# Moving the SBUF tiles that TensorE reads onto multiples of 512 bytes, with the low halves of the weight splits 32 bytes off

## The chip, the cores and the metric

One core of one Trainium2 chip. The metric is the device time of one execution in microseconds; the kernel before takes 1749.63 us, the median of three runs (1748.19 to 1751.73).

## The reference, cut to what matters

Two layers of a hybrid transformer over 256 latent and 256 context tokens, model width 1024. Each layer is half-step SwiGLU, attention in three groups of heads, half-step SwiGLU, each behind a modulated RMS norm. Nearly all of the arithmetic is fp32 matrix products:

```python
def _swiglu(u, w_gate, w_up, w_down):
    return (jax.nn.silu(u @ w_gate) * (u @ w_up)) @ w_down
...
h = h + 0.5 * g1 * _swiglu(_modulate(_rms_norm(h, norm_ffn1[l]), sh1, sc1),
                           w_ffn1_gate[l], w_ffn1_up[l], w_ffn1_down[l])
...
p = u @ w_in[l]
...
h = h + gm * (jnp.concatenate([y_w, y_g, y_n], axis=-1) @ w_out[l])
```

with w_gate and w_up of 1024 x 2816 and w_down of 2816 x 1024, for both token sets (the last layer drops the context after its keys and values).

## The kernel before, in words

Everything stands transposed: features on the 128 partitions, tokens along them. To keep fp32 accuracy with fp32r products, each operand is split in a high and a low part and three products are accumulated, high x high, high x low, low x high (`mm3`, L129 to L132). One product is one weight load (128 x 128) and one matmul over 256 or 512 tokens, so TensorE works through a list of pairs "load, matmul" in program order; the load of the next pair runs beside the matmul of this one.

- **Weights.** `wload` (L122 to L127) brings 512 KB from HBM on SP's queue into a `raw` tile (3 buffers), ScalarE copies it, rounded, into the high half of a `split` tile (4 buffers), VectorE writes the difference into the low half. `w` in `first_tiles` does the same for the first six tiles of the first layer, four of them in `split` buffers and the last two (`split0`) in buffers of the G tag.
- **Moving operands.** The normalised activations are `Uh` and `Ul` (high and low, pool acts). A feed-forward stage makes `pg` and `pu` from them (gate and up), then the hidden tiles `G` (high and low side by side), from which `pd` (down) is made and added to `H`. The names `pq`, `pk`, `pv`, `S` and `po` are the products of the mixer (queries, keys, values, scores, outputs); its output product is again called `pd`, from `Uh` and `Ul`.
- **Order.** The steps of the first tiles and of the mixers stand in lists written out by hand (`START`, `MIX`); the feed-forward stages run in loops: chunk by chunk gate and up, after each part the down products of the part before. VectorE takes the modulation jobs (`ascr`, L147) between its other work.
- **Where tiles lie.** A pool's tiles stand one behind the other, and a pool opened later begins where the last one ended, so an address follows from the sizes and the order in which the pools are opened. Counted in bytes from the start of a partition, the kernel before has:

```
consts   16512 .. 25280    ident at 16512
weights  25280 .. 70336    raw 3 x 4096, then split 4 x 8192 from 37568 (low half at +4096)
acts     70336 .. 119488   H 70336, Uh 86720, Ul 103104
norm    119488 .. 125920   acc, ms, rs, sq, t, hms, hrs
stage   125920 ..          one pool per stage: ffn1_0, mix_0, ffn2_0, ffn1_1, mix_1, ffn2_1
```

25280, 37568, 86720 and 103104 are all 192 past a multiple of 512 and so on a multiple of 64. In the first stage a `csel` tile (4096) and a `c2` tile (64) stand ahead of G, which begins at 130080, 32 past a multiple of 512; in the other feed-forward stages G begins at 125920, 480 past one. Both are 32 past a multiple of 64. The tiles of the mixers' pool that TensorE reads are 480 past a multiple of 512 ahead of the `sm` tiles (3 x 64 bytes) and 160 past one behind them, again 32 past one of 64. Steps inside a tile are multiples of 512 bytes throughout.

Of the kernel before, what the change touches and what calls it, by code (L numbers as in the profile page):

```python
# [10 lines left out]
F32 = mybir.dt.float32  # L11
F32R = mybir.dt.float32r
# [7 lines left out]
KT = D // 128  # L20
# [2 lines left out]
A_H, B_H, C_H = 6, 4, 6  # L23
ABUFS = 8
DV = 6
BANKS = {"mm": 3, "s": 2, "t": 2, "o": 1}
PIECES = 4
NT0 = 6
# [31 lines left out]
def hybrid_backbone(ctx: ExitStack, tc: tile.TileContext, I, out):  # L60
    nc = tc.nc
    ep = ctx.enter_context
    cp = ep(tc.tile_pool(name="consts", bufs=1))
    wp = ep(tc.tile_pool(name="weights", bufs=4))
    up = ep(tc.tile_pool(name="acts", bufs=1))
    npl = ep(tc.tile_pool(name="norm", bufs=2))
    psum = ep(tc.tile_pool(name="psum", bufs=1, space=bass.MemoryType.PSUM))

    def bank(tag, name):
        return psum.tile([128, 512], F32, tag=tag, name=name, bufs=BANKS[tag])  # L70

# [49 lines left out]

    def wload(src, n=1024):  # L122
        raw = raw_load(src, n)
        sp = wp.tile([128, 2, 1024], F32R, tag="split", name="split", bufs=4)
        act(sp[:, 0, :n], raw[:, :n], AF.Copy)  # L125
        tt(sp[:, 1, :n], raw[:, :n], sp[:, 0, :n].bitcast(F32), ALU.subtract)  # L126
        return sp  # L127
# [129 lines left out]
    def first_tiles(pool, csel, U, src):  # L257

        pss, sps, rb, ada_ps, ada_pt, rstd, tmp = [], [], [], {}, {}, {}, {}

        def r(h):
            if not rb:
                rb.append(bank("o", "rb"))
            rstd[h] = norm_rstd_stages(h, rb[0], 256 * h, "mm")
            next(rstd[h])

        def s(h):
            next(rstd[h], None)  # L270

        def a(p, i):

            if i == 0:
                ada_ps[p] = bank("mm", "adaps")
            c, b = divmod(i, 2)
            raw = pool.tile([128, 4, 256], F32, tag="araw", name="araw", bufs=ABUFS)
            nc.sync.dma_start(raw, I["w_ada0"][:, p, c, b])
            for j in range(4):
                mm(ada_ps[p][32 * j:32 * j + 32, :256], csel[:, 2 * j + b, c, :], raw[:, j, :], start=(i == 0),  # L280
                   stop=(i == 3))

        def b(p):
            sb = pool.tile([128, 256], F32, tag="adasb", name="adasb", bufs=1)
            act(sb, ada_ps[p][:, :256], AF.Copy)
            pt = ada_pt[p] = bank("mm", "adapt")
            for i in range(2):
                nc.tensor.transpose(pt[:, i * 128:(i + 1) * 128], sb[:, i * 128:(i + 1) * 128], ident)

        def c(p):  # L290
            v = ada_pt[p][:, :256].rearrange("p (b j r) -> p b r j", b=2, j=4)
            for i in range(2):
                f = i * KT + 2 * p
                nc.vector.tensor_reduce(ada[0][:, f:f + 2, :], v[:, :, 2 * i:2 * i + 2, :], axis=AX.X, op=ALU.add)
            for m in ("sh1", "sc1"):
                ada_fin(0, m, 2, slice(2 * p, 2 * p + 2))

        def w(i):
            raw = raw_load(src(i), 1024)
            if i < 4:  # L300
                t = wp.tile([128, 2, 1024], F32R, tag="split", name="split", bufs=4)
                parts = [(t, 0, 1024)]
            else:
                parts = [(pool.tile([128, 2, 512], F32R, tag="G", name="split0", bufs=10), o, 512) for o in (0, 512)]
            for t, o, n in parts:
                act(t[:, 0, :], raw[:, o:o + n], AF.Copy)
            sps.append((raw, parts))

        def x(i):
            raw, parts = sps[i]  # L310
            for t, o, n in parts:
                tt(t[:, 1, :], raw[:, o:o + n], t[:, 0, :].bitcast(F32), ALU.subtract)
            pss.append(bank(("s", "t", "s", "t", "mm", "mm")[i], "pf"))

        def u(f):
            shv = mod(0, "sh1")
            t2 = pool.tile([128, 2, TOK], F32R, tag="G", name="t0", bufs=10)[:, 0, :].bitcast(F32)
            for h in range(2):
                cols = (LAT, CT)[h]
                t = tmp[f, h] = t2[:, cols]  # L320
                stt(t, H[:, f, cols], amod[0][:, 0, f, h:h + 1], rb[0][:, 256 * h:256 * h + 256], op0=ALU.mult,
                    op1=ALU.mult)
                marks["act"] = ins_of(act(U[0][:, f, cols], t, AF.Identity, bias=shv[:, f, h:h + 1]))

        def v(f):
            shv = mod(0, "sh1")
            for h in range(2):
                cols = (LAT, CT)[h]
                stt(U[1][:, f, cols], tmp.pop((f, h)), shv[:, f, h:h + 1], U[0][:, f, cols].bitcast(F32),
                    op0=ALU.add, op1=ALU.subtract)  # L330

        def m(i, f):
            t, o, _ = sps[i][1][f // 4 if i >= 4 else 0]
            wh, wl = (t[:, e, f * 128 - o:f * 128 - o + 128] for e in range(2))
            mm(pss[i], wh, U[0][:, f, :], start=(f == 0), stop=False)
            mm(pss[i], wl, U[0][:, f, :], start=False, stop=False)
            mm(pss[i], wh, U[1][:, f, :], start=False, stop=(f == KT - 1))

        steps = dict(r=r, s=s, a=a, b=b, c=c, w=w, x=x, u=u, v=v, m=m)
        with tc.manual_schedule():  # L340
            for o in START.split():
                steps[o[0]](*map(int, o[1:]))
        return pss
# [105 lines left out]
    def mixer(l, pool, U):  # L449
# [158 lines left out]

        def scores(g):
            kd_, h, kd, (q, rs), e, v, vh = head_info(g)  # L610
            sm = pool.tile([128, 4, 4], F32, tag="sm", name="sm", bufs=3)
            nm, sums, es, rr = (sm[:, i, :] for i in range(4))
            P = []
            st[g] = P
# [201 lines left out]
    for l in range(DEPTH):  # L816
        last = l == DEPTH - 1
        with tc.tile_pool(name=f"ffn1_{l}", bufs=1) as pool:
            start = None
            if l == 0:  # L820
                csel = pool.tile([128, KT, 4, 32], F32, name="csel")
                nc.gpsimd.memset(csel, 0.0)
                c2 = pool.tile([128, KT, 2], F32, name="c2")
                nc.sync.dma_start(c2, I["ccol"])
                for h in range(2):
                    for i in range(2):
                        w = slice(4 * i, 4 * i + 4)
                        nc.sync.dma_start(H[:, w, (LAT, CT)[h]], I["xT"][:, w, (LAT, CT)[h]])
                for i in range(4):
                    act(csel[:, :, i, 2 * i:2 * i + 2], c2, AF.Silu)  # L830
                for h in range(2):
                    for d in range(KT):
                        norm_sq(h, d, nc.vector, pool)
                U = new_u()

                def start(chunk):
                    return first_tiles(pool, csel, U, chunk)
            if l == 0:
                jobs = [late_consts] + ada_jobs(0, ("g1", "shm", "scm", "gm", "sh2", "sc2"), pool)
            else:  # L840
                jobs = ada_jobs(1, ("shm", "scm"), pool) + ada_jobs(1, ("gm", "sh2", "sc2", "g2"), pool, 1)
            Um = []
            ffn(l, 1, (0, 1), pool, U, jobs, next_u(l, 1, Um), start)
            U = Um
        halves = (0,) if last else (0, 1)
        with tc.tile_pool(name=f"mix_{l}", bufs=1) as pool:
            Y, qcols = mixer(l, pool, U)
            Um = []
            out_proj(l, halves, Y, qcols, next_u(l, 2, Um))
            U = Um  # L850
        with tc.tile_pool(name=f"ffn2_{l}", bufs=1) as pool:
            if not last:
                jobs = ada_jobs(0, ("g2",), pool) + ada_jobs(1, ("sh1", "sc1", "g1"), pool)
            else:
                jobs = []
            Um = []

            def final(h):
                rb = norm_rstd(0)
                for i in range(4):  # L860
                    t = pool.tile([128, 2, 256], F32, tag="fin", name="fin", bufs=4)
                    for d in range(2):
                        stt(t[:, d, :], H[:, 2 * i + d, LAT], gains[:, 6, 2 * i + d:2 * i + d + 1], rb,
                            op0=ALU.mult, op1=ALU.mult)
                    (nc.sync, nc.scalar)[i % 2].dma_start(out[:, 2 * i:2 * i + 2, :], t)
                return []

            ffn(l, 2, halves, pool, U, jobs, final if last else next_u(1, 0, Um))
            U = Um
# [75 lines left out]
```

## Time and profile before

| | |
|---|---|
| median of 3 runs | 1749.63 us |
| the profiled execution's own time | 1749.41 us |
| span of its trace | 1747.2 us |
| TensorE (matmuls) busy | 1707.2 us, 98% |
| VectorE busy | 1180.4 us, 68% |
| ScalarE busy | 718.0 us, 41% |
| mean granted TensorE clock | 0.994 of full speed |

A matmul's record runs from its start to its modelled end, and the next one starts long before that end. So busy time says only that TensorE is never empty; how fast it works is read from the distance between the starts of neighbouring matmuls, in the timeline.

### The profile page before, as it was taken

The page shows a single profiled execution, that of the slowest core. Times are in us where ns is not written, and L with a number is a line of the kernel's source. Part 1 is how long each engine was busy: PE and PEld are TensorE (multiplying, and loading weights), DVE is VectorE, ACT ScalarE, POOL GpSimd, SP SyncE. Part 2 cuts the span into 40 slices and gives each one's busy share as a digit, 9 for nine tenths or more (in the row PEclk, how much of TensorE's full clock was granted, in tenths as well). Part 3 has the DMA queues.
Part 4 walks back from the last instruction along what each step waited for, and adds up shares of the span by engine and source line. Part 5 has one row for each costly group of instructions (what it writes and reads, how often), then busy time and mean ns, then how long its engine had stood idle before and what let it go on. Part 6 is the DMA issues. An engine that isn't in the chain of part 4 may idle for free.

```text
span 1747.2 us, 24756 instructions
## 1 busy us (share of the span) xinstructions
PE 1707.2 (98%) x9572; PEld 1473.6 (84%) x9572; DVE 1180.4 (68%) x2031; ACT 718.0 (41%) x1206; POOL 167.3 (10%) x251
## 2 busy tenths in 40 slices
PE   7999999999999999999999999999999999989997
PEld 4888888889888898888888988888888888889997
DVE  5899963447888869983334599944333797965555
ACT  4322222235888643222222442222222477754443
POOL 0311100002101031100000121200000210210000
PEclk9999999999999999999999999999999999999999
DMA  8877642323223247743324188923333233356663
GB/s 329 307 239 243 196 116 82 112 73 115 55 72 87 77 160 241 236 141 86 110 76 115 55 311 270 331 82 112 88 98 105 84 98 91 104 162 188 180 176 116
DMA packets 76693, 258.37 MB, mean 148 GB/s; under 512 B 8944, under 2 KB 11248, under 8 KB 76192
## 3 DMA queue, kind: packets, MB, share of 16 engines
q1 hardware_dynamic: 54096, 176.72, 33.1%
q0 software_dynamic: 21760, 79.38, 14.3%
q8 instruction: 75, 1.23, 0.3%
q10 hardware_dynamic: 720, 0.69, 0.1%
q14 instruction: 42, 0.34, 0.1%
HBM read 250.47 MB, written 1.05 MB: 144 GB/s over the span
## 4 chain that ended last, share of the span: by engine, by line
PE 89%; ACT 3%; DVE 3%; issue 2%; POOL 1%; DMA 1%; SPq 0%; POOLq 0%; DVEq 0%; ACTq 0%
PE pd L131 9%; PE pd L132 9%; PE pd L130 9%; PE pu L130 8%; PE pu L131 8%; PE pu L132 8%; PE pg L130 8%; PE pg L132 8%; PE pg L131 8%; PE pq L130 1%; PE pq L132 1%; PE pq L131 1%; PE pt L675 1%; PE pv L576 1%; PE pv L578 1%
## 5 line engine op out<-in xcount | busy, mean ns | idle before, releaser
L125 ACT ACTIVATE split<-raw 128x1024 fp32r<-128x1024 f32 (+1 forms) x336 | 332.8, 992 | 558.3 <-PE pd L132 235.3
L126 DVE TENSOR_TENSOR split<-raw,split 128x1024 fp32r<-128x1024 f32 (+1 forms) x336 | 382.9, 1140 | 235.4 <-ACT split L125 234.5
L147 DVE SCALAR_TENSOR_TENSOR ascr<-araw,cb 128x1024 f32<-128x1024 f32 x224 | 273.2, 1220 | 9.9 <-DMA araw<-in_w_adaT 5.7
L131 PE MATMUL pd<-G,split 128*128 128x512 f32 (+1 forms) x800 | 273.7, 343 | 0.0
L132 PE MATMUL pd<-G,split 128*128 128x512 f32 (+1 forms) x800 | 273.7, 343 | 0.0
L130 PE MATMUL pd<-G,split 128*128 128x512 f32 (+1 forms) x800 | 272.8, 343 | 0.0
L130 PE MATMUL pg<-Uh,split 128*128 128x512 f32 (+1 forms) x712 | 252.2, 355 | 2.1 <-ACT Uh L221 2.1
L132 PE MATMUL pg<-Uh,split 128*128 128x512 f32 (+1 forms) x712 | 251.9, 354 | 0.0
L130 PE MATMUL pu<-Uh,split 128*128 128x512 f32 (+1 forms) x712 | 251.9, 354 | 0.0
L131 PE MATMUL pu<-Ul,split 128*128 128x512 f32 (+1 forms) x712 | 251.8, 354 | 0.0
L131 PE MATMUL pg<-Ul,split 128*128 128x512 f32 (+1 forms) x712 | 251.6, 354 | 0.1
L132 PE MATMUL pu<-Uh,split 128*128 128x512 f32 (+1 forms) x712 | 251.7, 354 | 0.0
L230 DVE SCALAR_TENSOR_TENSOR H<-pd,ada,H 128x256 f32<-128x256 f32 x272 | 123.2, 478 | 112.3 <-PE pd L132 112.2
L131 PEld LDWEIGHTS pd<-G,split 128*128 128x128 f32 x800 | 150.2, 188 | 20.7
L130 PEld LDWEIGHTS pd<-G,split 128*128 128x128 f32 x800 | 149.7, 188 | 20.3
L132 PEld LDWEIGHTS pd<-G,split 128*128 128x128 f32 x800 | 150.1, 188 | 19.4
L130 PEld LDWEIGHTS pg<-Uh,split 128*128 128x128 f32 x712 | 134.9, 190 | 21.1 <-ACT Uh L221 2.6
L132 PEld LDWEIGHTS pg<-Uh,split 128*128 128x128 f32 x712 | 134.9, 189 | 18.7
L130 PEld LDWEIGHTS pu<-Uh,split 128*128 128x128 f32 x712 | 135.1, 190 | 18.4
L131 PEld LDWEIGHTS pg<-Ul,split 128*128 128x128 f32 x712 | 134.8, 190 | 18.7 <-DVE Ul L222 0.3
L132 PEld LDWEIGHTS pu<-Uh,split 128*128 128x128 f32 x712 | 134.9, 190 | 18.4
L131 PEld LDWEIGHTS pu<-Ul,split 128*128 128x128 f32 x712 | 134.9, 190 | 18.3
(199 smaller groups left out, 2415.2 us busy)
## 6 DMA issues: line engine op xcount, KB each, us to landing
araw<-in_w_adaT POOLq DMA_DIRECT2D x128, 512.0 KB, 5.1
raw<-in_w_ffn_gate SPq DMA_DIRECT2D x88, 512.0 KB, 4.0
raw<-in_w_ffn_up SPq DMA_DIRECT2D x88, 512.0 KB, 4.1
raw<-in_w_ffn_down SPq DMA_DIRECT2D x96, 384.0 KB, 3.3
raw<-in_w_in SPq DMA_DIRECT2D x26, 512.0 KB, 3.6
araw<-in_w_ada SPq DMA_DIRECT2D x16, 512.0 KB, 10.2
raw<-in_w_ffn_down SPq DMA_DIRECT2D x16, 512.0 KB, 3.7
raw<-in_w_out SPq DMA_DIRECT2D x16, 512.0 KB, 3.8
```

The lines of the kernel that those rows point to most:

```text
L125: act(sp[:, 0, :n], raw[:, :n], AF.Copy)
L126: tt(sp[:, 1, :n], raw[:, :n], sp[:, 0, :n].bitcast(F32), ALU.subtract)
L130: mm(ps, wh, xh, start=first, stop=False)
L131: mm(ps, wh, xl, start=False, stop=False)
L132: mm(ps, wl, xh, start=False, stop=last)
L147: stt(scr, raw, 1.0, cb[:, t, :], op0=ALU.mult, op1=ALU.mult, accum_out=ada[l][:, ft, t:t + 1])
L230: stt(H[:, d, cols], ps[:, off:off + 256], gate[:, d, half:half + 1], H[:, d, cols], op0=ALU.mult, op1=ALU.add)
L576: mm(ps[:, :n], U[0][:, k, c], s[:, 0, o:o + n], start=(k == 0), stop=False)
L578: mm(ps[:, :n], U[1][:, k, c], s[:, 0, o:o + n], start=False, stop=(k == KT - 1))
L675: nc.tensor.transpose(pt[:, k * 128:(k + 1) * 128], P[t][:, k * 128:(k + 1) * 128], ident)
```

## The change: the order of the pools, a filler, wider weight tiles

It opens the norm pool ahead of the weights, then a pool with one tile of 32 bytes that nothing uses, then weights and acts. The weight splits become 1032 elements wide per half, of which 1024 are used. Two small tiles, `sm` and `c2`, move from the stage pools to the norm pool, with the same number of buffers. No instruction is added or removed.

```diff
+FILL = 32
...
     cp = ep(tc.tile_pool(name="consts", bufs=1))
+    npl = ep(tc.tile_pool(name="norm", bufs=2))
+
+    fillp = ep(tc.tile_pool(name="filler", bufs=1))
+    fillp.tile([128, FILL], mybir.dt.uint8, name="fill")
     wp = ep(tc.tile_pool(name="weights", bufs=4))
     up = ep(tc.tile_pool(name="acts", bufs=1))
-    npl = ep(tc.tile_pool(name="norm", bufs=2))
...
-        sp = wp.tile([128, 2, 1024], F32R, tag="split", name="split", bufs=4)
+        sp = wp.tile([128, 2, 1032], F32R, tag="split", name="split", bufs=4)[:, :, :1024]
...
-                t = wp.tile([128, 2, 1024], F32R, tag="split", name="split", bufs=4)
+                t = wp.tile([128, 2, 1032], F32R, tag="split", name="split", bufs=4)[:, :, :1024]
...
-            sm = pool.tile([128, 4, 4], F32, tag="sm", name="sm", bufs=3)
+            sm = npl.tile([128, 4, 4], F32, tag="sm", name="sm", bufs=3)
...
-                c2 = pool.tile([128, KT, 2], F32, name="c2")
+                c2 = npl.tile([128, KT, 2], F32, name="c2", bufs=1)
```

By the same sums the norm pool then takes 25280 to 31968, the filler ends at 32000, `raw` takes 32000 to 44288, the four `split` tiles of 8256 bytes begin at 44288, 52544, 60800 and 69056 (256, 320, 384 and 448 past a multiple of 512, so each high half on a multiple of 64), each low half 4128 further (32 past a multiple of 64). `H` is at 77312, `Uh` at 93696, `Ul` at 110080 and the stage pools begin at 126464, all multiples of 512; and so are then `G`, `q`, `kd`, `vab`, `vc`, `pth` and `ptl`, and `split0`. `ident` stays where it was.

## Rows read from the trace of the kernel before

**Rows 1.** The page: busy time of each engine, share of the span, instructions

```profile
PE 1707.2 (98%) x9572; PEld 1473.6 (84%) x9572; DVE 1180.4 (68%) x2031; ACT 718.0 (41%) x1206; POOL 167.3 (10%) x251
```

**Rows 2.** Busy time by stretch: stretch, PE, PEld, DVE, ACT, POOL, clock, DMA share, GB/s

```profile
111.00:211.00 100.00, 100.00 (x439) 81.93 (x438) 99.06 (x162) 26.83 (x33) 13.98 (x26) 1.00 0.74 237
...
401.00:545.00 144.00, 142.62 (x879) 126.14 (x878) 117.12 (x253) 107.79 (x226) 17.26 (x18) 0.99 0.31 87
545.00:645.00 100.00, 96.20 (x635) 85.26 (x634) 80.08 (x158) 63.52 (x134) 18.76 (x23) 1.00 0.28 81
645.00:980.00 335.00, 335.00 (x1531) 277.48 (x1530) 203.34 (x307) 95.61 (x120) 14.84 (x29) 1.00 0.48 148
...
1377.00:1480.00 103.00, 99.36 (x653) 89.73 (x652) 84.49 (x179) 69.99 (x143) 11.09 (x11) 1.00 0.37 103
1480.00:1537.00 57.00, 55.42 (x401) 50.35 (x401) 51.98 (x99) 44.06 (x90) 13.64 (x15) 1.00 0.43 120
...
1587.00:1728.00 141.00, 141.00 (x1183) 140.82 (x1182) 84.46 (x111) 62.91 (x86) 0.00 (x0) 1.00 0.62 181
```

**Rows 3.** Span and mean granted TensorE clock of the core

```profile
core 0: 1747.2 us, clock 0.994
```

**Rows 4.** Groups of instructions by line and form, engine PE: busy us, mean ns

```profile
L130 PE MATMUL pg<-Uh,split 128*128 128x512 f32 x472 | 183.9, 390 | 0.0
...
L130 PE MATMUL pd<-G,split 128*128 128x512 f32 x432 | 170.3, 394 | 0.0
...
L130 PE MATMUL pd<-G,split 128*128 128x256 f32 x368 | 102.5, 282 | 0.0
...
L130 PE MATMUL pu<-Uh,split 128*128 128x256 f32 x240 | 68.3, 285 | 0.0
```

**Rows 5.** Timeline, engine PE, first feed-forward stage: start us, duration us, instruction

```profile
69.61 0.39 PE L130 MATMUL pg<-Uh,split 128*128 128x512 f32 x1
...
111.09 0.40 PE L130 MATMUL pd<-G,split 128*128 128x512 f32 x1
...
144.71 0.40 PE L130 MATMUL pg<-Uh,split 128*128 128x512 f32 x1
```

**Rows 6.** Timeline, engine PE: first tiles, and the start of the loop behind them

```profile
55.39 0.39 PE L337 MATMUL pf<-Ul,split 128*128 128x512 f32 x1
55.62 0.39 PE L335 MATMUL pf<-Uh,split 128*128 128x512 f32 x1
...
67.30 0.39 PE L337 MATMUL pf<-Ul,split 128*128 128x512 f32 x1
67.53 0.40 PE L130 MATMUL pg<-Uh,split 128*128 128x512 f32 x1
```

**Rows 7.** Timeline, engine PE, last feed-forward stage, matmuls of 256 columns

```profile
1639.01 0.28 PE L130 MATMUL pd<-G,split 128*128 128x256 f32 x1
...
1655.97 0.28 PE L130 MATMUL pg<-Uh,split 128*128 128x256 f32 x1
...
1659.93 0.28 PE L130 MATMUL pu<-Uh,split 128*128 128x256 f32 x1
...
1661.49 0.28 PE L131 MATMUL pu<-Ul,split 128*128 128x256 f32 x1
```

**Rows 8.** Timeline, engine PE, first mixer, output products of 256 columns

```profile
456.38 0.28 PE L684 MATMUL po<-pth,vab 128*128 128x256 f32 x1
...
456.71 0.28 PE L685 MATMUL po<-ptl,vab 128*128 128x256 f32 x1
```

**Rows 9.** The tiles sm and c2: instructions, and who waited (sm's reduction, c2's load)

```profile
L632 DVE TENSOR_REDUCE sm<-S x64: 671/680/693, 434.0 to 1517.2; 128x1 f32<-128x512 f32 x64
L824 SPq DMA_DIRECT2D c<-in_ccol x1: 390/390/390, 0.7 to 0.7; - x1
```

**Rows 10.** DMA issues in the first 45 us: median us to landing

```profile
araw<-in_w_ada SPq DMA_DIRECT2D x16, 512.0 KB, 10.2
H<-in_xT SPq DMA_DIRECT2D x4, 512.0 KB, 6.5
```

## The prediction, made before the changed kernel ran

> **What bounds the kernel.** I read the page's busy times first: TensorE is busy for 98% of the span, VectorE for 68%, ScalarE for 41% [rows 1]. Then the busy time by stretch: in the feed-forward stages TensorE has no gap at all (335.00 of 335.00 us, 141.00 of 141.00), in the mixer it has a few (96.20 of 100.00) [rows 2]. So what sets the time is how far apart TensorE's starts lie, times their number; nobody has to be waited for. The clock is no lever: 0.994 granted, which is the upper level, 2.4 GHz [rows 3].
>
> The duration of a matmul's record (390 ns) is no price, since the next one starts long before its end [rows 4]. The price is the distance of starts, read from the timeline over long stretches of one kind. In the first feed-forward stage, 183 matmuls on `Uh` and `Ul` run from 69.61 to 111.09: 41.48 / 183 = 226.7 ns each. The 144 on `G` that follow run to 144.71: 33.62 / 144 = 233.5 ns [rows 5]. Same columns, same weight loads, same engine, 6.8 ns apart. What differs in the code is the place: `Uh`, `Ul` and the weights are all on multiples of 64 bytes, `G` is 32 past one. In the first tiles it is the weights that are 32 off (`split0`) and the moving operand that is on a multiple: from 55.62 to 67.30, 50 matmuls at 233.6 ns [rows 6]. So a place 32 bytes apart between the two operands goes with the longer distance, whichever side it is on.
>
> With 256 columns it is turned round. On `U` 13 steps from 1659.93 to 1661.49 give 120.0 ns; on `G` 144 steps from 1639.01 to 1655.97 give 117.8 [rows 7]. Every one of these is over the columns' own time at 2.4 GHz (512 / 2.4 = 213.3, 256 / 2.4 = 106.7) by 11 to 20 ns, and that excess is all the change can reach.
>
> **The change part by part.** No instruction comes or goes, so each term is a count times a change of distance. Counts come from the groups by form; three lines (L130 to L132) have the same count, gate and up are two such sets [rows 4].
>
> 1. `G`, 512 columns: 3 x 432 = 1296. It comes to multiples of 512, and so stands to the high weight halves as `U` does now. I take the 226.7 of [rows 5]: 1296 x 6.8 = 8.8 us less. The bounds: 233.5 (nothing), and the 220 of the third rival below (17.5 less).
> 2. `U`, 512 columns: 2 x 3 x 472 = 2832. Moving operand and high halves stay on multiples of 64; the load of the low half, one in three, comes to lie 32 off. No row shows this mixture. The nearest one is its onset: the last matmul before the all-off stretch, during which the first off weights are loaded, takes 55.62 - 55.39 = 0.23 us against 0.227 [rows 6], so a single off load costs next to nothing. I take 0. Bounds: 231 (the unsettled starts behind that stretch: 67.53 to 69.61, nine steps, 231.1 [rows 5, 6]), 12.5 us more; and 220, 19 us less.
> 3. `U`, 256 columns: 2 x 3 x 240 = 1440. Of the rows with 256 columns the one with operands 32 apart is `G`'s, 117.8; I take it for the mixture, 1440 x 2.2 = 3.2 us less. Bounds: 110 from the best stretch of the mixer, where both sides are off by 32 (456.38 to 456.71, three steps [rows 8]), 14.4 less; and 120 plus the 6.9 that an offset costs at 512 columns, 9.9 more.
> 4. `G`, 256 columns: 3 x 368 = 1104. It has 117.8 now, and keeps it: 0. Bounds: 110 (8.6 less) and 120 (2.4 more).
> 5. Mixers and output products: four stretches of 404 us with 879 + 635 + 653 + 401 = 2568 matmuls [rows 2], broken by waits, so that only part of a shorter step arrives. At 2 ns for each it is 5 us if all arrived; I take 1 less, between 4 less and 4 more.
> 6. The moved `sm` and `c2`: same buffers, same instructions (the 64 reductions into `sm`, the one load of `c2` at 0.7 us [rows 9]), so no new wait; 0. The first loads (10.2 us to land [rows 10]) now write to multiples of 64 instead of 32 past one; no row shows the same load both ways, and I take 0, with 1 us either way.
>
> What covers the rest: VectorE is busy for 99.06 of 100 us from 111 to 211 [rows 2], though TensorE never waits for it there. If the `G` block that lies there (and half of the next; there are 1296 / 144 = 9) gets shorter, VectorE's splits may be late: up to 1.5 x 0.98 = 1.5 us of the first term would come back as a wait. I leave it in the range.
>
> Sum: 8.8 + 3.2 + 1.0 = 13.0 us less. The profiled execution took 1749.41 (0.2 under the median, which changes nothing), so 1736.4; by the milder bounds of terms 2 to 6, 1727 to 1744.
>
> **The rivals.**
>
> *Nothing happens (1749).* The 6.8 ns could belong to something else that goes with `G`: four PSUM writers, the accumulating `stt` on VectorE, the DMA traffic. Against it: `split0` shows the same 233.6 with `U` moving and no accumulation into `H` [rows 6]. It stays possible that a third of the loads being off eats what `G` gains. The Trainium skill ("TensorE: Matmul & The Clock Gate", Back-to-back issue gap) speaks for this rival: the isolated distance is columns / 2.4 + 2.5 ns, from the columns alone, so no address could matter. By that rule both kinds would stand at 215.8 ns before and after and the time would stay; the trace disagrees, with 226.7 and 233.5 for the same 512 columns [rows 5].
>
> *The low halves break the steady pace (slower, 1756).* Behind the off stretch it took nine matmuls at 231.1 until 226.7 was reached [rows 5, 6]; where every third load is off, it may never be reached. Then all 512-column steps run at 231.1: 2832 x 4.4 = 12.5 more, 1296 x 2.4 = 3.1 less, 256 columns and mixers 3.2 less as above: 6.2 more. It decides at 4128 x = 2832 x 226.7 + 1296 x 233.5 + 4200, that is x = 229.9 ns: a common distance above that loses. For it speaks that the mixture is shown nowhere; against it the cheap onset.
>
> *One step more (about 1695).* The steady distances 226.7 and 120.0 both lie 13.3 ns over the columns' time. If the off loads get out of the moving operand's way so that half of that goes (220 and 113.3), the sum is 2832 x 6.7 + 1296 x 13.5 + 1440 x 6.7 + 1104 x 4.5 = 51 us, with the mixers 54. For it speaks that 110 occurs [rows 8], against it that it holds for a few steps only.
>
> **How the numbers follow.** The forecast has 0.50, nothing 0.15, slower 0.20, one step more 0.15. Of the last I leave out the lower half and of the slower case what lies over 1757, together under 0.2: the range is 1708 to 1757. The forecast's own is 1727 to 1744. A measurement of this kernel can tell about 0.2% (3.5 us) from no change: faster by over that 0.65, within it 0.15, slower 0.20.
>
> **What would show it.** In the changed trace: 144 starts of `pd` from `G` at 226 to 227 ns instead of 233.5, `pg` and `pu` still at 226.7, the 256-column steps at or under 118, the same 9572 matmuls and no new wait for `split`. The prediction is wrong if `pg` and `pu` with 512 columns leave 226.7: up to 231, and the slower rival has it; down to 220, the last.

## The result, and the profile after

The change makes the kernel slower: 1760.72 us (median of four runs, 1759.15 to 1762.11) against 1749.87 in the same job, a ratio of 1.0064 with a 95% interval of 1.0051 to 1.0077. The profiled execution of after took 1759.15 us. Its page (busy us, share, instructions) and its core (span, clock):

```profile
PE 1715.2 (98%) x9572; PEld 1468.5 (84%) x9572; DVE 1182.3 (67%) x2031; ACT 718.4 (41%) x1206; POOL 166.7 (9%) x251
...
core 0: 1757.2 us, clock 0.995
```

The same 9572 matmuls, the same clock as [rows 1, 3], 10.0 us more of span. Busy time by stretch, after (columns as in [rows 2]):

```profile
111.00:211.00 100.00, 100.00 (x432) 80.89 (x431) 97.64 (x161) 25.84 (x32) 13.47 (x25) 1.00 0.73 231
...
645.00:980.00 335.00, 335.00 (x1510) 273.97 (x1509) 201.94 (x307) 94.83 (x120) 16.68 (x32) 1.00 0.48 148
...
1587.00:1728.00 141.00, 141.00 (x1197) 141.00 (x1196) 85.03 (x113) 64.11 (x89) 0.00 (x0) 1.00 0.65 186
```

TensorE is still never empty in the feed-forward stages. In the same 335 us it now starts 1510 matmuls in place of 1531 [rows 2]; in the last stage, with 256 columns, 1197 in place of 1183. So the loss is with 512 columns and is partly given back with 256. The waits of TensorE (engine, line, waited for: us in total, times, longest), before and then after:

```profile
PE ss L197 <- DVE acc L189: 12.8, 3, 9.9
PE rb L206 <- POOL rs L202: 7.2, 10, 1.0
...
PE pv L577 <- DVE split L126: 0.6, 1, 0.6
```

```profile
PE ss L201 <- DVE acc L193: 12.7, 3, 9.4
PE rb L210 <- POOL rs L206: 7.2, 10, 1.0
...
PE pv L581 <- DVE split L130: 1.8, 2, 1.1
```

The long ones are the same. One in the mixer, `pv` for `split`, grew by 1.2 us; in the kernels below it is between nothing and 1.5 us, and whether the change made it stays open. In the feed-forward stages nothing waits for `split` but the first tiles, 1.7 us before and after.

The timeline of after, engine PE (start us, duration us, instruction), at the ends of blocks of one kind:

```profile
109.88 0.39 PE L134 MATMUL pd<-G,split 128*128 128x512 f32 x1
...
143.29 0.39 PE L134 MATMUL pg<-Uh,split 128*128 128x512 f32 x1
...
148.88 0.39 PE L134 MATMUL pu<-Uh,split 128*128 128x512 f32 x1
...
154.47 0.39 PE L134 MATMUL pg<-Uh,split 128*128 128x512 f32 x1
...
160.02 0.39 PE L134 MATMUL pu<-Uh,split 128*128 128x512 f32 x1
...
165.57 0.39 PE L134 MATMUL pg<-Uh,split 128*128 128x512 f32 x1
...
210.13 0.39 PE L134 MATMUL pd<-G,split 128*128 128x512 f32 x1
...
1598.82 0.28 PE L134 MATMUL pd<-G,split 128*128 128x256 f32 x1
...
1615.78 0.27 PE L134 MATMUL pg<-Uh,split 128*128 128x256 f32 x1
...
1649.80 0.28 PE L134 MATMUL pd<-G,split 128*128 128x256 f32 x1
```

- 144 steps on `G`: 109.88 to 143.29, 33.41 / 144 = 232.0 ns (before 233.5 [rows 5]).
- 288 steps on `U`: 143.29 to 210.13, 66.84 / 288 = 232.1 ns (before 226.7 [rows 5]).
- Within these, one weight tile is 24 steps, and the four buffers of `split` come in turn: 5.59, 5.59, 5.55 and 5.55 us, that is 232.9, 232.9, 231.3 and 231.3 ns. The buffers differ, and all four are slow.
- 256 columns: `G` 16.96 / 144 = 117.8 ns as in [rows 7]; `U` 34.02 / 288 = 118.1 ns (before 120.0 [rows 7]).

Over the whole trace, from the distance of neighbouring starts (those within 32 ns of the columns' own time), before to after: `U` with 512 columns 227.34 to 232.07 (3349 of them), `G` with 512 233.38 to 232.04 (1296), `U` with 256 119.83 to 118.10 (2280), `G` with 256 117.84 to 117.95 (1073), `po` 117.00 to 118.84 (286). The products are +15.8, -1.7, -3.9, +0.1 and +0.5 us: +10.8, against 10.0 between the spans of the two traces and 10.85 between the medians. By stretch, the feed-forward stages (first to last `pg`) took 10.6 us more and those between them 1.7 more; what lies ahead of the loop's first `pg` took 2.2 less (67.53 before, 65.32 after).

### The profile page after: what moved, and what is told of

Its sections match the earlier page's. It is cut to its first block, busy times and chain, and to the rows that moved or that the text cites. A ratio compares the mean times of both kernels' runs of the same rounds, so it can differ in the third digit from the quotient of the medians.

```text
span 1757.2 us, 24756 instructions
## 1 busy us (share of the span) xinstructions
PE 1715.2 (98%) x9572; PEld 1468.5 (84%) x9572; DVE 1182.3 (67%) x2031; ACT 718.4 (41%) x1206; POOL 166.7 (9%) x251
## 4 chain that ended last, share of the span: by engine, by line
PE 88%; DVE 4%; ACT 3%; issue 2%; DMA 1%; POOL 1%; POOLq 0%; DVEq 0%; SPq 0%; ACTq 0%
PE pd L135 8%; PE pd L134 8%; PE pd L136 8%; PE pu L135 8%; PE pu L134 8%; PE pg L135 8%; PE pg L134 8%; PE pu L136 8%; PE pg L136 8%; PE pq L134 1%; PE pq L136 1%; PE pq L135 1%; PE pt L679 1%; PE pv L580 1%; PE pv L581 1%
## 5 line engine op out<-in xcount | busy, mean ns | idle before, releaser
L136 PEld LDWEIGHTS pd<-G,split 128*128 128x128 f32 x800 | 150.2, 188 | 18.9
```

The costliest lines, as they stand in the source:

```text
L136: mm(ps, wl, xh, start=False, stop=last)
```

## The experiments

Distances between places are counted in bytes modulo 256 from here on; why, the bare pairs show. "Weights 64 past" means that the weights stand 64 bytes further than the moving operand, modulo 256.

### One part alone, and everything on one place

**Only the wider weight tile, in the kernel before** (pools in their old order):

```diff
-        sp = wp.tile([128, 2, 1024], F32R, tag="split", name="split", bufs=4)
+        sp = wp.tile([128, 2, 1032], F32R, tag="split", name="split", bufs=4)[:, :, :1024]
```

(and the same for `t` in `first_tiles`).

> The kernel before with the wider split tiles alone: order of pools as before, low halves 32 bytes off the high ones, U and the high halves on multiples of 64, G 32 past one as before. Theory P (low halves break the steady pace): the 512-column steps on U go from 227.3 to about 232 as in the changed kernel, 3349 x 4.7 = 15.8 us more, those with 256 columns 3.9 us less; G has two off loads in three instead of three, 233.4 or slightly less; 1761 us, as the changed kernel or up to 2 us above it. Rival R (the moving of pools to multiples of 512 cost the time, not the low halves): 1750, with U at 226.7.

Measured: 1762.81 us, ratio 1.0069 (1.0054 to 1.0084), the time that theory P had. Timeline of this kernel:

```profile
113.17 0.40 PE L130 MATMUL pd<-G,split 128*128 128x512 f32 x1
...
146.62 0.40 PE L130 MATMUL pg<-Uh,split 128*128 128x512 f32 x1
...
213.46 0.40 PE L130 MATMUL pd<-G,split 128*128 128x512 f32 x1
```

`G` 33.45 / 144 = 232.3, `U` 66.84 / 288 = 232.1: the wide tile alone brings all of the loss. More than the low halves moved, though: the tile is 8256 bytes, so three of the four high halves moved too: they stand 64, 128 and 192 past `Uh` and `Ul`. Which of the two it is, the last experiments take apart.

**The change without the wider tile**, so that moving operand and both halves stand on one place:

```diff
-FILL = 32
+FILL = 288
...
-        sp = wp.tile([128, 2, 1032], F32R, tag="split", name="split", bufs=4)[:, :, :1024]
+        sp = wp.tile([128, 2, 1024], F32R, tag="split", name="split", bufs=4)
```

> The changed kernel without the wider splits: the filler is 288 bytes instead of 32, so that splits too, both halves, begin on multiples of 512, and everything else lies where it does in the changed kernel. Theory P: every 512-column step on U and G settles at 226.7 and every 256-column one at 120.0. Against the kernel before: G at 512 columns 1296 x 6.7 = 8.7 us less, G at 256 columns 1073 x 2.2 = 2.3 us more, output products of the mixer 288 x 3 = 0.9 more: 1744 to 1745. Rival R (moving the pools is what cost): 1757 to 1761.

Measured: 1741.87 us, ratio 0.995 (0.9935 to 0.9964), 2 to 3 us under what theory P had, and far from rival R. Timeline of this kernel:

```profile
108.99 0.39 PE L134 MATMUL pd<-G,split 128*128 128x512 f32 x1
...
141.63 0.39 PE L134 MATMUL pg<-Uh,split 128*128 128x512 f32 x1
...
206.91 0.39 PE L134 MATMUL pd<-G,split 128*128 128x512 f32 x1
...
1578.74 0.28 PE L134 MATMUL pd<-G,split 128*128 128x256 f32 x1
...
1596.02 0.28 PE L134 MATMUL pg<-Uh,split 128*128 128x256 f32 x1
```

512 columns: 32.64 / 144 = 226.7 on `G` and 65.28 / 288 = 226.7 on `U`. 256 columns: 17.28 / 144 = 120.0 on `G`. So one place for all is the best of the kernels so far with 512 columns and the worst with 256. The wider tile costs 1760.72 - 1741.87 = 18.9 us on top of this layout.

**Both halves of the weights 32 off** (480 past a multiple of 512, moving operands on multiples):

```diff
-FILL = 32
+FILL = 256
...
+    fill2 = ep(tc.tile_pool(name="filler2", bufs=1))
+    fill2.tile([128, 32], mybir.dt.uint8, name="fill2")
     up = ep(tc.tile_pool(name="acts", bufs=1))
...
-        sp = wp.tile([128, 2, 1032], F32R, tag="split", name="split", bufs=4)[:, :, :1024]
+        sp = wp.tile([128, 2, 1024], F32R, tag="split", name="split", bufs=4)
```

> The changed kernel with both halves of each split 32 bytes off a multiple of 64 (splits 480 past a multiple of 512), a second filler bringing the moving tiles back to multiples of 512. Theory P: all products with splits have their operands 32 apart, like G in the kernel before: 512 columns at 233.4 on U and G, 256 columns at 117.8. Against the kernel before 3349 x 6.1 = 20.4 us more, 2283 x 2.0 = 4.6 us less, 0.9 more in the mixer's output products: 1766. Rival S (only the mixture within one triple costs; loads that are all off alike settle at 226.7): about 1741 to 1745, as with all on multiples of 512.

Measured: 1764.67 us, ratio 1.0074 (1.0056 to 1.0092), near theory P's 1766 and not rival S's 1741 to 1745. Timeline of this kernel:

```profile
112.11 0.39 PE L136 MATMUL pd<-G,split 128*128 128x512 f32 x1
...
145.72 0.39 PE L136 MATMUL pg<-Uh,split 128*128 128x512 f32 x1
...
212.91 0.39 PE L136 MATMUL pd<-G,split 128*128 128x512 f32 x1
...
1606.39 0.28 PE L136 MATMUL pd<-G,split 128*128 128x256 f32 x1
...
1623.35 0.28 PE L136 MATMUL pg<-Uh,split 128*128 128x256 f32 x1
```

33.61 / 144 = 233.4 on `G`, 67.19 / 288 = 233.3 on `U`, 16.96 / 144 = 117.8 with 256 columns: the pace that `G` has in the kernel before, now on `U` too. The distance goes with the place of the two operands against each other and not with the tile's name, its PSUM bank or what reads the result.

### Bare pairs: the distance against the place, and nothing else running

A kernel of loads and matmuls alone, in segments of one layout each; `m` and `ws` are the bytes by which moving operand and weights stand past a multiple of 512:

```python
def seg(n, reps, m, ws, m_cols=128, mstep=512):
    for j in range(reps):
        a = m // 4 + (j % 4) * mstep
        w = ws[j % len(ws)] // 4 + (j // len(ws) % 4) * 128
        nc.tensor.matmul(ps[:m_cols, :n], wt[:, w:w + m_cols], mv[:, a:a + n], start=(j == 0), stop=(j == reps - 1))
```

> This kernel leaves the whole computation out: it is one list of load-and-matmul pairs, 33 segments with 512 columns (48 pairs each) and the same 33 with 256 columns (72 pairs each), with no other engine at work; only the byte places of the weights and of the moving operand differ from segment to segment. Theory P (the distance of starts is set by the place of the weights being loaded against the place of the moving operand): same place 226.7 ns at 512 columns and 120.0 at 256; 32 bytes apart about 233.3 and 117.8, whichever side is moved; both moved by 32 together 226.7 and 120.0 again; one load in three 32 off 230 to 233 and 118, as in the changed kernel. By its wider form the places count modulo 64, so 64 apart is again 226.7; by its narrower form modulo 128 or more, so 64 apart is something else. If the excess over the columns' time is the load reading beside the matmul, weights of 64 and 32 columns bring 226.7 down towards 220 and 217. Rival Q (the surroundings of G set its distance: accumulation into H, PSUM readers, DMA writes): all segments of one width show the same distance, 226.7 and 120.0 or the bare 215.8 and 109.2, whatever the place.

> The whole computation is left out again: bare load-and-matmul pairs, 512 columns and then 256, first with the moving operand at every 16th byte from 0 to 240 and the weights at 0, then weights at eight places and the moving operand at 0, then triples as in the kernel (two moving tiles and two weight halves at places of their own). Theory P in its wider form (places count modulo 64): the distance repeats after 64 bytes. In its narrower form (modulo 256, after 64 and 128 apart were unlike 0 and 256 apart was like it): no repeat within the 256. Settling (whether a segment reaches the short pace depends also on where it starts): the same place in two segments can give two distances. Triples: low half 32 off 230 to 233.4 at 512 columns, as in the changed kernel; no triple with different places is expected under 226.7.

Measured, one execution of each of the two kernels, mean distance of starts in the second half of a segment, in ns (two values: two segments of the same layout):

| layout | 512 columns | 256 columns |
|---|---|---|
| same place (0 and 0, or both 32 past) | 226.7 | 120.0 |
| weights 256 past | 226.7 | 120.0 |
| weights 16 past | 226.7 and 233.3 | 118.3 |
| weights 32 past | 233.4 | 118.3 |
| weights 64 past | 233.5 and 233.2 | 117.8 and 113.3 |
| weights 320 past | 233.4 | 113.3 |
| weights 112 past | 233.3 | 120.0 |
| weights 128 past | 232.4 | 118.7 |
| weights 192 past | 229.0 | 113.3 |
| weights 448 past | 228.8 | 113.3 |
| moving operand 16 past | 231.6 to 231.9 | 113.3 or 118.7 |
| moving operand 32 past | 233.3 | 116.7 |
| moving operand 64 past | 228.8 or 233.4 | 113.3 or 117.8 |
| moving operand 96 past | 233.2 and 233.4 | 120.0 |
| moving operand 112 past | 231.4 | 113.3 |
| moving operand 240 past | 226.7 | 117.1 |
| weights in turn 0, 32, 0 | 233.4 | 118.3 |
| weights in turn 64, 96, 64 | 230.9 | 118.9 |
| same place, weights of 64 columns | 230.0 | 113.3 |
| same place, weights of 32 columns | 231.7 | 113.3 |

Four whole segments of the first kernel, 48 loads each, in the columns of [rows 2]: same place, weights 32 past, weights 64 past, weights in turn 0, 32, 0:

```profile
24.43:35.31 10.88, 10.88 (x49) 9.01 (x48) 0.00 (x0) 0.00 (x0) 0.00 (x0) 1.00 0.01 2
35.32:46.50 11.18, 11.18 (x49) 9.01 (x48) 0.00 (x0) 0.00 (x0) 0.00 (x0) 1.00 0.00 0
101.24:112.43 11.19, 11.19 (x49) 9.02 (x48) 0.00 (x0) 0.00 (x0) 0.00 (x0) 1.00 0.00 0
289.45:300.63 11.18, 11.18 (x49) 9.01 (x48) 0.00 (x0) 0.00 (x0) 0.00 (x0) 1.00 0.01 1
```

Four things follow. With no other engine at work and next to no DMA the distances of the kernel are there: 226.7, 233.4, 120.0, 118; rival Q is out. Multiples of 64 are not alike: 64 apart costs as much as 32, and of those tried only 256 is as good as 0, while 320 is like 64 and 448 like 192. The direction counts: the moving operand 112 past has 231.4 and 113.3, the weights 112 past 233.3 and 120.0. And 232 is no mean of good and bad loads: one load in three off gives 233.4, as much as all three. What fell is the thought that the excess is the part of a weight load which the moving operand holds up: a load of a quarter of the columns is no faster with 512 columns (231.7), though it is with 256 (113.3).

Some layouts have two values. To see what picks between them, each was started twelve times, every time behind three matmuls of 4 columns more than the last time. At 2.4 GHz that is 1.67 ns for each of the three, so about 5 ns together, not the 1.67 that the expectation names. Theory U had the start pick among patterns that repeat themselves, V one of them for each place:

> The whole computation is left out: six choices of places, each twelve times, and ahead of each of the twelve three matmuls of 264, 268, ... 308 columns, which shift the moment at which the segment starts by 1.67 ns a time. Theory U (each choice of places has several self-repeating patterns of distances, and the start picks one): the moving operand 64 past the weights, 256 columns: some of the twelve at 113.3 and some at 117.8; 16 past: some at 113.3, some at 118.7; same place: all twelve at 120.0 and at 512 columns all or nearly all at 226.7; low half alone 32 off, 512 columns: 230 to 233.4, never 226.7; all 32 off: 233.3 in all twelve. Rival V (the places alone decide, and the two values seen for one choice came from the segments before): all twelve alike.

Measured: moving operand 64 past, 256 columns: 117.8 in eleven starts, 113.35 in one; 16 past: 118.6 to 118.8 in six, 113.3 in four, 116.7 and 120.0 in one each. Same place: 226.7 and 120.0 in all twelve. Low half 32 off, 512 columns: 233.6 in all twelve (steps of about 228, 233 and 239 ns in turn, which is 233.3 over whole turns); all 32 off: 233.2 to 233.4 in all twelve. So U: the place gives the set of patterns, and where there are several, the start picks one. The two that matter for the change, 226.7 and 233.4, have no second value in twelve starts.

### Can both column counts have their best place?

One place for all is best with 512 columns and worst with 256, and the last layer's end works on 256 columns of tiles that are 512 wide. So these kernels take the kernel with everything on one place and put those 256 columns further on:

```diff
+OFF = slice(16, 272)
...
+        uc = OFF if l == 1 and n == 2 else cols
...
+        mc = cols if both else OFF
...
-            act(g[:, 0, cols], sil[:, cols], AF.Copy)
-            tt(g[:, 1, cols], sil[:, cols], g[:, 0, cols].bitcast(F32), ALU.subtract)
+            act(g[:, 0, mc], sil[:, cols], AF.Copy)
+            tt(g[:, 1, mc], sil[:, cols], g[:, 0, mc].bitcast(F32), ALU.subtract)
...
+        zc = qcols if l == 0 else OFF
```

(`uc`, `mc` and `zc` then stand for `cols` wherever `U`, `G` and the last output product's `Z` are written and read.) The offset was 64 bytes as above, then 16 with `slice(4, 260)`, then 112 with `slice(28, 284)`.

> The kernel with everything on multiples of 512 (1741.87), and in the last layer, where only 256 of the 512 columns of U and G are used from the output product on, those 256 stand 16 columns (64 bytes) further, so that every moving operand there is 64 bytes past the weights' place. Theory P with what the bare segments showed (113.3 ns with the moving operand 64 bytes past the weights, 120.0 at the same place): 1056 gate and up, 528 down and 192 output products go from 119.9 to 113.3: 1776 x 6.6 = 11.7 us less, 1730. Rival T (in the full kernel weight chunks, ScalarE or VectorE end later than a faster TensorE, so the step does not arrive): 1738 to 1742, with waits for split in the last stage.

> As the kernel with the 64-byte shift in the last layer, with 4 columns (16 bytes) instead of 16. Theory U: 113.3 ns (1730) if the stage happens to start into it, else 118.7 against 119.9, that is 1776 x 1.2 = 2 us under 1741.9: 1740. Rival V: the 64-byte shift's result, 1738.

> The same with 28 columns (112 bytes). Theory U: 113.3 ns (1730) if the stage starts into it; if not, between 117 and 120: 1738 to 1742. Rival V: the 64-byte shift's result, 1738.

| offset | median us | ratio to before (95%) | last stage, distance |
|---|---|---|---|
| 0 (above) | 1741.87 | 0.995 (0.9935 to 0.9964) | 120.0 |
| 64 bytes | 1738.46 | 0.9937 (0.9921 to 0.9954) | 117.8 |
| 16 bytes | 1736.45 | 0.9923 (0.9906 to 0.9939) | 116.7 |
| 112 bytes | 1733.04 | 0.9901 (0.9886 to 0.9915) | 113.3 |

The distances are those of the profiled executions. At 64 bytes 1730 had been forecast and missed: the stage settled on 117.8, the slower of the two values of the bare pairs. That is the time of rival T, but not its cause, since TensorE has no wait for `split` in that stage. At 16 bytes the 116.7 is a value that one of the twelve starts had too; the four times lie between 1734.21 (the profiled one) and 1737.82, and which value the others had was not seen. At 112 bytes the stage has 113.3 in every block, and rival V's 1738 is out; whether other starts would give it another value there was not tried. Timeline of the kernel with 112 bytes, and its only wait of TensorE for `G`:

```profile
1578.35 0.28 PE L135 MATMUL pd<-G,split 128*128 128x256 f32 x1
...
1594.67 0.28 PE L135 MATMUL pg<-Uh,split 128*128 128x256 f32 x1
```

```profile
PE pd L135 <- ACT G L376: 0.6, 1, 0.6
```

16.32 / 144 = 113.3 ns. The stage shrinks from 192.1 to 182.5 us, 9.6 where its 1584 products times 6.7 ns are 10.6; 0.6 of the rest is that wait, which the kernel without offset does not have: with this pace ScalarE's work becomes late there. At 1733.04 us it is the fastest version that was run, 27.7 us under the changed kernel. The moving operand 240 past, with 226.7 and 117.1 the one place in the table that is good with 512 columns and not the worst with 256, was tried in no kernel; the same distance set from the other side, weights 16 past, had 226.7 in one segment and 233.3 in another.

### Which half does it: the low half's 32, or the buffers' 64?

Two kernels made from the changed one. In the first every high half has the moving operand's place and every low half is 32 past it (the halves in two pools of four 4096-byte buffers, 32 bytes between the pools):

```diff
+class Pair:
+    def __init__(self, hp, lp):
+        self.t = (hp.tile([128, 1024], F32R, tag="split", name="split", bufs=4),
+                  lp.tile([128, 1024], F32R, tag="splitl", name="splitl", bufs=4))
...
-        sp = wp.tile([128, 2, 1032], F32R, tag="split", name="split", bufs=4)[:, :, :1024]
+        sp = Pair(wp, wlp)
```

In the second the low half has its high half's place, and the buffers step on by 64 as in the changed kernel:

```diff
-        sp = wp.tile([128, 2, 1032], F32R, tag="split", name="split", bufs=4)[:, :, :1024]
+        sp = wp.tile([128, 2064], F32R, tag="split", name="split", bufs=4)[:, :2048].rearrange("p (i n) -> p i n", i=2)
```

> The changed kernel with every high half of the weights on the same place as the moving operand (counted modulo 256 bytes) and every low half 32 past it; in the changed kernel the wide tile also moves the four buffers on by 64 each, so three of four high halves stand 64, 128 or 192 away. Theory L (the low half's 32 bytes alone do it): nothing moves, U with 512 columns stays at 232.1 ns, about 1761 us. Theory S (the steps of 64 between buffers alone do it): 226.7 and 120.0 ns as with everything on one place, about 1742 us. Theory P (each operand's place counts, as in the bare pairs): the bare triple with only its low half 32 off had 233.4 and 118.3 ns, so U and G with 512 columns at 233.4 (3349 x 1.3 + 1296 x 1.4 = 6.2 us more) and some 1 us more with 256 columns, about 1768 us, and no difference between the buffers.

> The changed kernel with each low half 4096 bytes behind its high half in place of 4128, so on the same place as its high half modulo 256; the buffers still step on by 64. Theory L: 226.7 and 120.0 ns everywhere, about 1742 us. Theory S: as the changed kernel, 232.1 ns, about 1761 us. Theory P: the four buffers differ as the bare pairs 0, 64, 128 and 192 apart did (226.7, 233.4, 232.4, 229.0 with 512 columns; 120.0, 113.3 or 117.8, 118.7, 113.3 with 256), a mean near 230.4 with 512 (4645 x 1.7 = 7.8 us less than the changed kernel) and 116 to 117.5 with 256 (2 to 7 us less): 1746 to 1751 us, and one buffer in four at 226.7.

Measured: 1779.27 us, ratio 1.0173 (1.0159 to 1.0187), for the low halves' 32 alone; 1754.93, ratio 1.0034 (1.0021 to 1.0048), for the buffers' 64 alone. Timeline of the first, at the starts of five weight tiles in a row:

```profile
145.53 0.40 PE L150 MATMUL pg<-Uh,split 128*128 128x512 f32 x1
...
151.13 0.40 PE L150 MATMUL pu<-Uh,split 128*128 128x512 f32 x1
...
156.74 0.40 PE L150 MATMUL pg<-Uh,split 128*128 128x512 f32 x1
...
162.34 0.40 PE L150 MATMUL pu<-Uh,split 128*128 128x512 f32 x1
...
167.94 0.40 PE L150 MATMUL pg<-Uh,split 128*128 128x512 f32 x1
```

And of the second:

```profile
144.61 0.40 PE L134 MATMUL pg<-Uh,split 128*128 128x512 f32 x1
...
150.08 0.40 PE L134 MATMUL pu<-Uh,split 128*128 128x512 f32 x1
...
155.67 0.39 PE L134 MATMUL pg<-Uh,split 128*128 128x512 f32 x1
...
161.26 0.39 PE L134 MATMUL pu<-Uh,split 128*128 128x512 f32 x1
...
166.76 0.39 PE L134 MATMUL pg<-Uh,split 128*128 128x512 f32 x1
```

In the first all four buffers have 5.60 / 24 = 233.3 ns. In the second they have 5.47, 5.59, 5.59 and 5.50 us, or 227.9, 232.9, 232.9 and 229.2 ns, where the bare pairs 0, 64, 128 and 192 apart had 226.7, 233.4, 232.4 and 229.0. So theory P: each operand's place counts, L and S both fall, and either part of the wide tile alone makes the kernel slower than before. The two don't add up: together, as in the change, they give 232.1, less than the 32 alone. By buffer, the change has 232.9, 232.9, 231.3 and 231.3, so over the second kernel the low halves' 32 add 5.0 ns where the high half is on the moving operand's place, and 0, -1.6 and 2.1 where it is off already.

Theory P's times were too low, though: 1768 and 1746 to 1751 had been forecast. Of the first kernel's 18.6 us over the changed one, the stretches from the first to the last `pg` of the feed-forward stages hold 1205.3 - 1196.5 = 8.8 (7 had been forecast); the stretches between them, with the mixers, hold another 8.6 (478.6 against 470.0). That kernel also keeps the halves as two tiles, and whether its mixers lose by that or by the places was not tried. In the second the 512-column steps gave 230.8 on average for the 230.4 expected, the 256-column ones 117.8 for 116 to 117.5.

## Why the prediction was wrong

The bound was read rightly: distance of starts times their number explains the result within a microsecond, and of the waits only one moved by more than a microsecond. By the steps:

- **Term 2 (`U`, 512 columns: 0) is the step that failed.** It took 0 on two premises, and both fail. The first: high halves and moving operand "stay on multiples of 64". [Rows 5, 6] only show operands on the same place (both 192 past a multiple of 256) against operands 96 apart (192 and 32 past), not 32 as the prediction has it. That any multiple of 64 is as good as the same place was added to them, and it does not hold: with the buffers' steps of 64 alone, those 64, 128 and 192 past have 232.9, 232.9 and 229.2. The second: a single off load "costs next to nothing". It rests on the onset, 0.23 us against 0.227, one record in a view of 10 ns steps, which cannot tell 226.7 from 233; and one step does not show a pattern that repeats. (The 50 steps of [rows 6] also hold three of a `split` tile on the moving operand's place, 59.83 to 60.51; the other 47 have 234.1. No term changes by it.) With the low halves' 32 alone every step is 233.3. The term measured 232.1, just above its upper bound of 231: on its own 2832 matmuls 15.0 us more in place of none, from 226.8 (15.8 with the mixers' 512-column products on `U`).
- **Term 1 (`G`, 512 columns: 8.8 less)** fell with it: "as `U` does now" is true of one buffer in four. `G` reads the same weights as `U`, so it came to 232.0 and not 226.7, 1.7 us less. With everything on one place it has the 226.7 that the term expected, so the reading of `G` was right and the weights' side of it was missed.
- **Term 3 (`U`, 256 columns)** was right: 118.1 for the forecast 117.8. That an offset helps there although it hurts at 512 was read from [rows 7] and holds in the bare pairs.
- **Term 4** (`G`, 256) kept 117.8, as forecast. **Term 5**: the stretches between the feed-forward stages went from 468.3 to 470.0 us, 1.7 more for 1 less, within its bounds. **Term 6**: no new wait for `sm` or `c2`, right; the wait of `pv` for `split` is 1.8 us in place of 0.6.
- **VectorE as the next bound** could not show in the change, since `G` got hardly faster: 97.64 of 100 us busy, for 99.06 [rows 2]. With everything on one place `G` did reach 226.7, and no wait for `split` came in the loops of the feed-forward stages: the 1.5 us put aside for it would not have been needed.
- **The rivals.** The slower one had half of the mechanism, low halves that keep the pace from coming back to 226.7, and its decision point, 229.9; its 231.1 became 232.1, worth 4128 x 1.0 = 4.1 us, which is why the time lies over its 1756 and over the range's end at 1757. That it came so near is in part luck: the low halves alone give 233.3, and the buffers' steps of 64, which no rival names, are the other half. Its nine steps at 231.1 have operands on one place; they show that the pace behind an off stretch comes back late, not what a mixture costs. It deserved more than the 0.20 all the same: the unknown mixture had been priced by its cheapest row, one onset. *Nothing happens* is out, and with it a distance from the columns alone: with 512 columns and 128-column weights the bare pairs have 226.7 to 234.8. The Trainium skill ("TensorE: Matmul & The Clock Gate", Back-to-back issue gap) gives columns / 2.4 + 2.5 ns, 215.8 for 512 columns, for an isolated matmul and not for a stream of loads and matmuls; no run here shows that figure. *One step more* did not come; 113.3 with 256 columns does exist, but at other places (the moving operand 112 past the weights, for one), and no block or segment with 512 columns had 220.

What in the chip makes the distance depend on the place stays open. The runs show that it does, with TensorE alone at work, and not why.

## What to carry to other kernels

Where a kernel is bound by TensorE without a gap, read the distance of starts per block of one kind before anything else, and compare blocks of equal shape: a few ns there were worth more here than any wait that was left. Place moving operand and weights by their distance modulo 256 bytes, its direction included, for every buffer of a rotating tile and every part in it, and measure it per column count (these runs show it for fp32r operands with 512 and 256 columns, no more); padding a tile changes the step from buffer to buffer as well as the offset inside. A premise such as "multiples of 64 are alike" is to be held against the rows: do they show two different multiples, or only one?

## What the runs showed that was not expected

- The same place is the best for 512 columns (226.7) and, with 120.0, as slow as any for 256; weights 32 past it is 233.4 and 118.3, moving operand 112 past 231.4 and 113.3. No place that was tried has the best of both.
- Segments settle into patterns that repeat. The three that have one step only, 226.7, 120.0 and 113.3, are 34, 18 and 17 times 6.67 ns; why, no run shows. The bare triple with its low half 32 off repeats 228, 233 and 239 ns, to within 1 ns, in all twelve starts.
- Where a place has more than one pattern, a start some ns later can pick another: 16 apart with 256 columns gave 113.3 in four of twelve starts and 118.6 to 118.8 in six.
- At the same place narrower weights make the steps longer with 512 columns (230.0 and 231.7 for 64 and 32 columns, against 226.7) and shorter with 256 (113.3).
